# Gate logits ahead of the token mixers, as two-by-two blocks with seven products for eight

## Chip, core and metric

The kernel runs on one core of one Trainium2 chip. The metric is the device time of one execution, in microseconds; 2918.35 us is the median of three runs before the change (2917.76 to 2919.18).

## The reference

One decoder layer in float32, 512 tokens, model width 2048. The part that the change touches is the hybrid mixer: one input projection of 12560 columns, whose last 3 x 2048 columns are the logits of three gates, and the merge of three branches by these gates.

```python
proj = xn @ w_in                                  # xn: 512 x 2048
dn_qkv, dn_z, dn_a, dn_b, swa_q, swa_kv, sb_qkv, gates = split_cols(proj, IN_SIZES)
...                                               # y_dn (1024), y_swa (512), y_sb (512)
gate = jax.nn.sigmoid(gates).reshape(bsz, seq, N_BRANCH, D_MODEL)
merged = gate[:, :, 0] * (y_dn @ w_br_dn) + gate[:, :, 1] * (y_swa @ w_br_swa) + gate[:, :, 2] * (y_sb @ w_br_sb)
return merged @ w_o
```

After it come the cross attention into 256 memory tokens, a convolutional FFN and the final norm, which the change leaves alone.

## The kernel before

Activations lie feature-major: a tile holds 128 features by 512 tokens, and the normalized input xn is 16 such tiles, each kept as a sum of two tiles of the fast 32-bit matmul type, `hi` and `lo` (called xh and xl in the code). A dense product of 128 output features is `dense`: for each of 16 k-tiles of the weights, three matmuls of 512 columns add wh x hi, wh x lo and wl x hi into one PSUM bank. The weights come as 512 KB `raw` tiles on SP's queue (three buffers); for four k-tiles at a time ScalarE (ACT) casts wh, and VectorE (DVE) forms wl = raw - wh (four buffers each). These loads, casts and subtractions have high priority, so the scheduler that orders each engine's instructions puts them well ahead of their use; it fixes one order per engine, and an engine takes its instructions in that order.

The stages are: transposes of mem and x with the memory projections on PE (until about 84 us), the gated DeltaNet, sliding window and stick-breaking attention (four heads, to about 853 us), the merge (region `p_c`, to about 1557 us), output projection, cross attention, FFN. In the merge, for each of 16 output tiles m and each branch b, the gate's dense product of 48 matmuls runs, ACT takes its sigmoid into `sg`, then the branch's dense product of 8, 4 or 4 k-tiles runs, DVE multiplies the two, and POOL adds the branches. The branch inputs y (16 tiles, y15 from the last stick-breaking head) are split into yh and yl at m = 0. The gate products depend on xn alone, so the scheduler places the first of them between the steps of the last stick-breaking head. In that head `z` are the scores (L651), `ops` the output (L686).

PSUM has eight banks: `acc` (two) for dense products, `gps` (six in the attention stage) for all else.

Of the kernel before, what the change touches and what calls it, by code (L numbers as in the profile page):

```python
# [17 lines left out]
P = 128  # L18
# [40 lines left out]
def decoder_kernel(ctx: ExitStack, tc: tile.TileContext, x, mem, norm_mix, w_in, dn_conv, dn_a_log, dn_dt_bias, dn_norm,  # L59
# [11 lines left out]
    main = ctx.enter_context(tc.tile_pool(name="main", bufs=1))  # L71
    rawp = ctx.enter_context(tc.tile_pool(name="rawp", bufs=3))
    wsp = ctx.enter_context(tc.tile_pool(name="wsp", bufs=4))
    misc = ctx.enter_context(tc.tile_pool(name="misc", bufs=2))
    psd = ctx.enter_context(tc.tile_pool(name="psd", bufs=2, space=bass.MemoryType.PSUM))
    psum = ctx.enter_context(ExitStack())
    gen = []

    def gen_pool(name, bufs):
# [5 lines left out]
    def dense_ps():  # L85
        return psd.tile([P, S], F32, name="acc")
# [11 lines left out]

# [1 line left out]
    def constant(where, name, col, w=P, queue=nc.gpsimd):  # L100
# [18 lines left out]
    hi = [None] * KT  # L119
    lo = [None] * KT  # L120

    def split_slot(k):
        hi[k] = main.tile([P, S], F32R, name=f"hi{k}")
        lo[k] = main.tile([P, S], F32R, name=f"lo{k}")
        return hi[k], lo[k]

    def mrg_tile(k):
        return main.tile([P, S], F32, name=f"mrg{k}")

# [42 lines left out]

# [121 lines left out]
    gen_pool("psg_dn", 3)  # L294
    y = [None] * 16
    with region("p_dn") as dp:
# [90 lines left out]
        for h0 in range(0, DNH, 2):  # L387
# [25 lines left out]
            act.activation(dt, dt, AF.Exp)  # L413
            # keys
            kd, junk = wide("kd"), dp.tile([P, P], BF16, name="junk", bufs=1)
# [39 lines left out]
            for lvl in range(LEVELS):  # L455
# [94 lines left out]

# [1 line left out]
    with tc.issue_after(last.ins):  # L552
# [137 lines left out]

# [1 line left out]
    mrg = [None] * KT  # L692
    with region("p_c") as cp:
        yh, yl = [None] * 16, [None] * 16
        for m in range(KT):
            for b, (w, k0, nk) in enumerate(((w_br_dn, 0, 8), (w_br_swa, 8, 4), (w_br_sb, 12, 4))):
                acc = dense_ps()
                dense(acc, w_in, 0, KT, O_G + b * D + m * P, xh, xl)
                sg = misc.tile([P, S], F32, name="sg")
                last = act.activation(sg, acc, AF.Sigmoid)  # L700
                if m == 0:
                    for k in range(k0, k0 + nk):
                        yh[k] = cp.tile([P, S], F32R, name=f"yh{k}", bufs=1)
                        yl[k] = cp.tile([P, S], F32R, name=f"yl{k}", bufs=1)
                        split(yh[k], yl[k], y[k])
                acc = gen_ps()
                dense(acc, w, 0, nk, m * P, yh[k0:k0 + nk], yl[k0:k0 + nk])
                if b == 0:
                    mrg[m] = mrg_tile(m)
                    dve.tensor_tensor(mrg[m], acc, sg, op=ALU.mult)  # L710
                else:
                    t = misc.tile([P, S], F32, name="m0")
                    dve.tensor_tensor(t, acc, sg, op=ALU.mult)  # L713
# [4 lines left out]
    def token_rstd(sq, o, t):  # L718
# [24 lines left out]
    with region("p_e") as ep:  # L743
# [25 lines left out]
        for h in range(4):  # L769
# [37 lines left out]
            ol.append(l_)  # L807
# [1 line left out]
    NCH = 4  # L809
    with region("p_g") as gp:  # L810
# [20 lines left out]
        def up_pair(j):  # L831
            res = []
            for s, c in enumerate((j, 32 + j)):
                acc = dense_ps()
                dense(acc, w_up, 0, KT, c * P, hh, hl)
                v = gp.tile([P, S], F32, name="v")
                dve.tensor_tensor(v, acc, rstd, op=ALU.mult)  # L837
                u = gp.tile([P, S], F32, name="u", bufs=3)
                act.activation(u, v, AF.Copy, scale=ffcw[:, 128 + c:129 + c])  # L839
                for i in (1, 0):  # L840
                    sh = 2 - i
                    w = ffcw[:, 64 * i + c:64 * i + c + 1]
# [6 lines left out]
            where, tags = (main, (f"mrg{2 * n}", f"mrg{2 * n + 1}")) if n < 8 else (gp, (f"ah{n}", f"al{n}"))  # L849
# [97 lines left out]
```

## Time and profile before

| | |
|---|---|
| median of three runs | 2918.35 us (2917.76 to 2919.18) |
| the profiled execution | span 2917.2 us; as the runs go some 1.2 us more in its own time |
| granted TensorE clock, mean | 0.996 |
| busy share PE / DVE / ACT / POOL | 98% / 45% / 36% / 9% |
| merge stage, 853 to 1558 us | 3105 matmuls of 512 columns |
| HBM | 266.41 MB read, 4.19 MB written, 93 GB/s over the span |

In the lines of the profile, L153 is line 153 of the kernel above. A row of the groups gives line, engine, operation, output tile and input tiles, shapes, how often, then the busy time in us, the mean duration in ns, and the idle time ahead with the engine that ended it. A row of the timeline begins with the start and the duration in us; a row with xN joins N neighbours. Matmuls overlap: one of 512 columns lasts 0.39 us, but the next may start before it ends, and the distance from start to start is what counts.

### The profile page before, as it was taken

How to read it: one execution, taken by the hardware profiler on the slowest of the kernel's cores; microseconds unless marked ns; L12 is line 12 of the kernel's file. 1: busy time of each engine (PE TensorE's matmuls, PEld its weight loads, DVE VectorE, ACT ScalarE, POOL GpSimd, SP SyncE). 2: the span in 40 equal slices, each digit the busy share in tenths (PEclk: the TensorE clock that was granted, in tenths of full speed). 3: DMA queues.
4: the chain of work that ended last, by engine and by line, in shares of the span. 5: the costliest groups of instructions: out<-in, count | busy, mean ns of one | idle time of the engine just before them, and what ended most of it. 6: DMA issues, size and time to landing. Idle time of an engine off the chain costs nothing.

```text
span 2917.2 us, 34620 instructions
## 1 busy us (share of the span) xinstructions
PE 2867.7 (98%) x13463; PEld 2365.3 (81%) x13463; DVE 1322.4 (45%) x2305; ACT 1046.6 (36%) x1926; POOL 260.0 (9%) x195
## 2 busy tenths in 40 slices
PE   7999999999999999999999999999999999999998
PEld 7787887877778888888888887788888888888887
DVE  7466576336334223223224344544344434443445
ACT  6444344334443222222224334533223323322333
POOL 2100010100000000000000110201001000000002
PEclk9999999999999999999999999999999999999999
DMA  6322212232223333333334432333333333333333
GB/s 206 103 65 73 56 53 73 64 86 65 73 76 98 94 98 98 94 98 98 94 98 124 118 97 73 91 97 99 95 101 94 99 97 94 101 94 96 99 94 116
DMA packets 469941, 272.84 MB, mean 94 GB/s; under 512 B 11249, under 2 KB 450018, under 8 KB 469138
## 3 DMA queue, kind: packets, MB, share of 16 engines
q1 hardware_dynamic: 468576, 268.60, 32.4%
q8 instruction: 105, 1.72, 0.2%
q0 software_dynamic: 560, 1.79, 0.2%
q14 instruction: 58, 0.48, 0.0%
q10 hardware_dynamic: 642, 0.26, 0.0%
HBM read 266.41 MB, written 4.19 MB: 93 GB/s over the span
## 4 chain that ended last, share of the span: by engine, by line
PE 88%; DVE 3%; ACT 1%; issue 1%; POOL 1%; ACTq 0%; DVEq 0%; POOLq 0%
PE acc L155 21%; PE acc L153 21%; PE acc L154 21%; PE gps L875 4%; PE gps L873 4%; PE gps L874 4%; PE gps L153 2%; PE gps L155 2%; PE gps L154 2%; PE gps L471 1%; PE gps L466 1%; DVE wl L150 1%; PE gps L593 0%; PE gps L686 0%; PE gps L651 0%
## 5 line engine op out<-in xcount | busy, mean ns | idle before, releaser
L153 PE MATMUL acc<-hi,wh 128*128 128x512 f32 x2912 | 1140.8, 392 | 0.7 <-ACT hi L132 0.7
L154 PE MATMUL acc<-lo,wh 128*128 128x512 f32 x2912 | 1141.2, 392 | 0.0
L155 PE MATMUL acc<-hi,wl 128*128 128x512 f32 x2912 | 1141.2, 392 | 0.0
L150 DVE TENSOR_TENSOR wl<-raw,wh 128x512 fp32r<-128x512 f32 x826 | 589.0, 714 | 940.5 <-ACT wh L149 917.9
L149 ACT CAST wh<-raw 128x512 fp32r<-128x512 f32 x840 | 521.7, 622 | 1304.7 <-PE acc L154 1093.0
L155 PEld LDWEIGHTS acc<-hi,wl 128*128 128x128 f32 x2912 | 547.9, 188 | 113.0 <-issue 2.3
L153 PEld LDWEIGHTS acc<-hi,wh 128*128 128x128 f32 x2912 | 547.6, 188 | 113.3 <-issue 1.6
L154 PEld LDWEIGHTS acc<-lo,wh 128*128 128x128 f32 x2912 | 547.8, 188 | 111.6 <-issue 0.9
L868 DVE TENSOR_TENSOR wl<-raw,wh 128x512 fp32r<-128x512 f32 x112 | 77.7, 694 | 165.2 <-ACT wh L867 145.0
L867 ACT CAST wh<-raw 128x512 fp32r<-128x512 f32 x112 | 69.8, 623 | 206.7 <-PE gps L874 171.9
L875 PE MATMUL gps<-wl,mrg 128*128 128x512 f32 x368 | 143.3, 389 | 0.0
L873 PE MATMUL gps<-wh,mrg 128*128 128x512 f32 x368 | 143.2, 389 | 0.0
L874 PE MATMUL gps<-wh,mrg 128*128 128x512 f32 x368 | 143.2, 389 | 0.0
L847 POOL TENSOR_TENSOR u<-u 128x512 f32<-128x512 f32 x32 | 58.3, 1823 | 900.8 <-ACT wh L149 801.2
L714 POOL TENSOR_TENSOR mrg<-mrg,m 128x512 f32<-128x512 f32 x32 | 52.2, 1632 | 641.9 <-DVE m L713 641.9
L843 DVE SCALAR_TENSOR_TENSOR u<-v,ffcw,u 128x511 f32<-128x511 f32 (+1 forms) x128 | 96.1, 751 | 14.6 <-ACT u L839 12.3
L153 PE MATMUL gps<-yh,wh 128*128 128x512 f32 x256 | 99.8, 390 | 0.0
L155 PE MATMUL gps<-yh,wl 128*128 128x512 f32 x256 | 99.7, 389 | 0.0
L154 PE MATMUL gps<-yl,wh 128*128 128x512 f32 x256 | 99.7, 389 | 0.0
L837 DVE TENSOR_TENSOR v<-acc,rstd 128x512 f32<-128x512 f32 x64 | 44.3, 692 | 100.5 <-PE acc L155 100.5
L875 PEld LDWEIGHTS gps<-wl,mrg 128*128 128x128 f32 x368 | 69.1, 188 | 14.4
L874 PEld LDWEIGHTS gps<-wh,mrg 128*128 128x128 f32 x368 | 69.1, 188 | 14.3
(425 smaller groups left out, 2537.0 us busy)
## 6 DMA issues: line engine op xcount, KB each, us to landing
raw<-in_w_in_dram SPq DMA_DIRECT2D x196, 512.0 KB, 3.8
raw<-in_w_up_dram SPq DMA_DIRECT2D x128, 512.0 KB, 4.0
raw<-in_w_down_dram SPq DMA_DIRECT2D x64, 512.0 KB, 3.8
raw<-in_w_o_dram SPq DMA_DIRECT2D x32, 512.0 KB, 4.1
raw<-in_w_xkv_dram SPq DMA_DIRECT2D x16, 512.0 KB, 5.0
raw<-in_w_br_dn_dram SPq DMA_DIRECT2D x16, 512.0 KB, 4.0
xraw<-in_x_dram SPq DMA_DIRECT2D x4, 1024.0 KB, 9.3
raw<-in_w_br_swa_dram SPq DMA_DIRECT2D x16, 256.0 KB, 2.7
```

The lines of the kernel that those rows point to most:

```text
L149: act.copy(wh, raw[:, s0:s0 + 4, :])
L150: (pool if share and s0 else dve).tensor_tensor(wl, raw[:, s0:s0 + 4, :], wh.bitcast(F32), op=ALU.subtract)
L153: pe.matmul(acc, wh[:, j, :], hs[k], start=(k == 0), stop=False)
L154: pe.matmul(acc, wh[:, j, :], ls[k], start=False, stop=False)
L155: pe.matmul(acc, wl[:, j, :], hs[k], start=False, stop=(k == nk - 1))
L843: dve.scalar_tensor_tensor(u[:, sh:S], v[:, 0:S - sh], w, u[:, sh:S], op0=ALU.mult, op1=ALU.add)
L847: pool.tensor_tensor(res[0], res[0], res[1], op=ALU.mult)
L867: act.copy(wh, raw[:, i, :])
L868: dve.tensor_tensor(wl, raw[:, i, :], wh.bitcast(F32), op=ALU.subtract)
L873: pe.matmul(acc, ah[j][:, ts], wh, start=(k == 0), stop=False)
L874: pe.matmul(acc, al[j][:, ts], wh, start=False, stop=False)
L875: pe.matmul(acc, ah[j][:, ts], wl, start=False, stop=(k == 7))
```

## The change

A new stage `p_gate` stands between the memory projections and the DeltaNet. It computes all gate logits and sigmoids and stores them to DRAM; the merge loads each 256 KB gate tile back as `sg` instead of computing it. The 16 k-tiles fall into two halves, an output pair is 256 columns of weights (two tiles of 128), and the 512 tokens fall into two halves of 256. So a pair is a two-by-two block product, done with seven block products of eight k-tiles (Winograd's form of Strassen's scheme). Each block product has per k-tile one matmul of 512 columns, wh with the moving block's hi and lo parts side by side, and one of 256 columns, wl with hi. The hi and lo results lie in two halves of a bank, which `fold` adds.

Four of the moving blocks are differences of quarters of xn. They are formed once, into fb0 to fb7, on DVE and ACT at the stage's start. Three of the weight blocks are the raw weights' (sraw, 1 MB each, three buffers), the others sums and differences that DVE forms per pair (`combine`, tiles sm). swh and swl, the split of 8 k-tiles at once (1024 columns), have two buffers each. The pair's banks sa, sb, sc, sd have two buffers each: all of PSUM. So the pools of the dense products (mrgp, rawp, wsp, psd) are closed before the stage and opened again behind it, and the stage's tiles use their memory. `misc` tile s7 is named sg, as the merge's loaded gates are. hi and lo of one k-tile are now halves of one tile x.

```diff
     def split_slot(k):
-        hi[k] = main.tile([P, S], F32R, name=f"hi{k}")
-        lo[k] = main.tile([P, S], F32R, name=f"lo{k}")
+        both = main.tile([P, 2, S], F32R, name=f"x{k}")
+        hi[k], lo[k] = both[:, 0, :], both[:, 1, :]
+        xb[k] = both
...
+    psum.close()
+    std.close()
+    HT = S // 2
+    gate_d = [[None] * KT for _ in range(3)]
+    with region("p_gate") as gp, tc.tile_pool(name="psw", bufs=2, space=bass.MemoryType.PSUM, reuse_waits="tile") as pw:
+        fb = [gp.tile([P, 2, 4, HT], F32R, name=f"fb{k}", bufs=1) for k in range(8)]
+        banks = {n: [pw.tile([P, S], F32, name=n) for _ in range(2)] for n in ("sb", "sd")}
+        for n in ("sb", "sd"):
+            for t in banks[n]:
+                pe.matmul(t, xh[0][:, 0:P], xh[0], start=True, stop=True)
+        for k in range(8):
+            u = gp.tile([P, 2, S], F32, name="g")
+            for j in range(2):
+                dve.tensor_tensor(u[:, j, :], xh[k + 8 * j].bitcast(F32), xl[k + 8 * j].bitcast(F32), op=ALU.add)
+            b11, b12, b21, b22 = (u[:, j, t * HT:(t + 1) * HT] for j in range(2) for t in range(2))
+            v = gp.tile([P, 4, HT], F32, name="sm")
+            for i, (p_, q_) in enumerate(((b12, b11), (b22, v[:, 0, :]), (b22, b12), (b21, v[:, 1, :]))):
+                dve.tensor_tensor(v[:, i, :], p_, q_, op=ALU.subtract)
+            act.copy(fb[k][:, 0, :, :], v)
+            dve.tensor_tensor(fb[k][:, 1, :, :], v, fb[k][:, 0, :, :].bitcast(F32), op=ALU.subtract)
...
+        def product(acc, w, of, first):
+            wh = gp.tile([P, 8, P], F32R, name="swh")
+            wl = gp.tile([P, 8, P], F32R, name="swl")
+            with tc.high_priority(1000000):
+                act.copy(wh, w)
+                dve.tensor_tensor(wl, w, wh.bitcast(F32), op=ALU.subtract)
+            av = acc.rearrange("p (h c) -> p h c", h=2)
+            for k in range(8):
+                m = of(k)
+                pe.matmul(av, wh[:, k, :], m, start=(first and k == 0), stop=False, skip_group_check=True)
+                pe.matmul(av[:, 0, :], wl[:, k, :], m[:, 0, :], start=False, stop=(k == 7), skip_group_check=True)
...
+            a, b, c, d = (pw.tile([P, S], F32, name=n) for n in ("sa", "sb", "sc", "sd"))
+            product(a, a11, B11, True)
+            act.copy(b, a)
+            product(c, combine(a11, a21, ALU.subtract), T3, True)
+            s1 = combine(a21, a22, ALU.add)
+            s2 = combine(s1, a11, ALU.subtract)
+            s7 = misc.tile([P, S], F32, name="sg")
+            act.copy(s7, c)
+            product(b, s2, T2, False)
+            product(a, a12, B21, False)
+            act.copy(d, b)
+            la = gp.tile([P, HT], F32, name="la")
+            act.copy(la, a[:, HT:S])
+            fold(out[:, 0, 0:HT], a[:, 0:HT], la)
+            product(d, s1, T1, False)
+            t = misc.tile([P, S], F32, name="m0")
+            dve.tensor_tensor(t, d, s7, op=ALU.add)
+            fold(out[:, 1, HT:S], t[:, 0:HT], t[:, HT:S])
+            product(b, a22, T4, False)
...
+            product(d, combine(a12, s2, ALU.subtract), B22, False)
...
+        for m in range(0, KT, 2):
+            for b_ in range(3):
+                g = gp.tile([P, 2, S], F32, name="g")
+                strassen_pair(w_in, O_G + b_ * D + m * P, g)
+                act.activation(g, g, AF.Sigmoid)
+                gd = dram.tile([P, 2, S], F32, name=f"gate{b_}_{m}")
+                pool.dma_start(out=gd, in_=g)
+                gate_d[b_][m], gate_d[b_][m + 1] = gd[:, 0, :], gd[:, 1, :]
...
-                acc = dense_ps()
-                dense(acc, w_in, 0, KT, O_G + b * D + m * P, xh, xl)
                 sg = misc.tile([P, S], F32, name="sg")
-                last = act.activation(sg, acc, AF.Sigmoid)
+                nc.sync.dma_start(out=sg, in_=gate_d[b][m])
```

How the order of the instructions changes is shown at three places. The first is DVE behind the memory projections. Before, the last weight splits of these (L150) led over to the DeltaNet's first ones:

```order
L275 COPY rsb<-gps 128x256
L150 TENSOR_TENSOR wl<-raw,wh 128x512 x2
L310 TENSOR_TENSOR wh<-raw,wh 128x8x16 x2
L150 TENSOR_TENSOR wl<-raw,wh 128x512 x4
L326 TENSOR_TENSOR abt<-gps,abt 128x64
```

Now the combined blocks stand there, some 50 rows for eight k-tiles, of which these are the first of the second and third (fb_1036 is fb0, x_518 and x_582 the xn tiles 2 and 10):

```order
L317 TENSOR_TENSOR fb_1036<-sm,fb_1036 128x1024
L315 TENSOR_TENSOR sm<-g,sm 128x256
L311 TENSOR_TENSOR g<-x_518 128x512
L334 TENSOR_TENSOR swl<-sraw,swh 128x1024
L315 TENSOR_TENSOR sm<-g,sm 128x256
L311 TENSOR_TENSOR g<-x_582 128x512
L315 TENSOR_TENSOR sm<-g 128x256 x2
L317 TENSOR_TENSOR fb_1037<-sm,fb_1037 128x1024
```

Between fb0's row and the swl of the second product stand 12 operations of L311, 26 of L315, 7 of L317, the swl of the first product and one combine.

The second place is a gate's work on DVE. Before, in the merge, a tile's three multiplications with the weight splits between them:

```order
L710 TENSOR_TENSOR mrg_7763<-gps,sg 128x512
L150 TENSOR_TENSOR wl<-raw,wh 128x512 x5
L713 TENSOR_TENSOR m_7855<-gps,sg 128x512
L150 TENSOR_TENSOR wl<-raw,wh 128x512 x5
L713 TENSOR_TENSOR m_7948<-gps,sg 128x512
```

Now one pair of the new stage, from the swl of its second product (first row) to that of its seventh (last row):

```order
L334 TENSOR_TENSOR swl<-sm,swh 128x1024
L342 TENSOR_TENSOR g<-sd,la 128x256
L357 TENSOR_TENSOR sm<-sm,sraw 128x1024
L334 TENSOR_TENSOR swl<-sm,swh 128x1024
L334 TENSOR_TENSOR swl<-sraw,swh 128x1024
L334 TENSOR_TENSOR swl<-sm,swh 128x1024
L357 TENSOR_TENSOR sm<-sraw,sm 128x1024
L357 TENSOR_TENSOR sm<-sraw 128x1024
L334 TENSOR_TENSOR swl<-sraw,swh 128x1024
L342 TENSOR_TENSOR g<-sa,la 128x256
L376 TENSOR_TENSOR m_1958<-sd,sg 128x512
L334 TENSOR_TENSOR swl<-sm,swh 128x1024
```

The combine in the third row is s2, which stands behind swl of the second product and a fold of the pair before; c7 and the next pair's c2 (L357, seventh and eighth row) stand ahead of swl of the sixth product. The same stretch on ACT, from the next pair's first and second cast on; the sigmoid of the pair before stands ahead of the third product's cast:

```order
L333 CAST swh<-sraw 128x1024
L333 CAST swh<-sm 128x1024
L384 COPY la<-sd 128x256
L391 ACTIVATE g<-g 128x1024
L362 COPY sb<-sa 128x512
L333 CAST swh<-sm 128x1024
L333 CAST swh<-sraw 128x1024
L367 COPY sg<-sc 128x512
```

L362 is the copy b<-a of the new pair; the third product's cast (sixth row) stands behind it and the sigmoid.

The third place is PE in the last stick-breaking head. Before, matmuls of the first gate filled the steps of the head (the rows on hi and lo are the gate's):

```order
L640 MATMUL gps<-ident,svt 128x128 x4
L153 MATMUL acc<-hi_497,wh 128x512
L154 MATMUL acc<-lo_498,wh 128x512
L155 MATMUL acc<-hi_497,wl 128x512
L651 MATMUL gps<-sq,sk 128x512
L651 MATMUL gps<-sq,sk 128x384
L651 MATMUL gps<-sq,sk 128x256
L153 MATMUL acc<-hi_506,wh 128x512
```

Now the head's rows follow one another (L764 scores, L783 to L792 the sums, L799 the output), and the first branch product comes behind the last; the rows between are left out here after the first of them:

```order
L753 MATMUL gps<-ident,svt 128x128 x4
L764 MATMUL gps<-sq,sk 128x512
L764 MATMUL gps<-sq,sk 128x384
L764 MATMUL gps<-sq,sk 128x256
L764 MATMUL gps<-sq,sk 128x128
L783 MATMUL gps<-sph,tri_lr 128x512
```

```order
L799 MATMUL gps<-sz,svv 128x512
L799 MATMUL gps<-sz,svv 128x384
L799 MATMUL gps<-sz,svv 128x256
L799 MATMUL gps<-sz,svv 128x128
L165 MATMUL acc<-yh_11340,wh 128x512
```

Nothing of the dense work is left that depends on xn alone, so the places between are empty.

More of the change, by code (lines that the diff above doesn't have):

```diff
@@ L71, in decoder_kernel, with open_std @@
     main = ctx.enter_context(tc.tile_pool(name="main", bufs=1))
-    rawp = ctx.enter_context(tc.tile_pool(name="rawp", bufs=3))
-    wsp = ctx.enter_context(tc.tile_pool(name="wsp", bufs=4))
     misc = ctx.enter_context(tc.tile_pool(name="misc", bufs=2))
-    psd = ctx.enter_context(tc.tile_pool(name="psd", bufs=2, space=bass.MemoryType.PSUM))
+    dram = ctx.enter_context(tc.tile_pool(name="dram", bufs=1, space=bass.MemoryType.DRAM))
+    std = ctx.enter_context(ExitStack())
     psum = ctx.enter_context(ExitStack())
     gen = []
+    mrgp = rawp = wsp = psd = None
+    def open_std(n):
+        nonlocal mrgp, rawp, wsp, psd
+        psum.close()
+        std.close()
+        mrgp, rawp, wsp = (std.enter_context(tc.tile_pool(name=f"{name}{n}", bufs=bufs, reuse_waits="tile"))
+                           for name, bufs in (("mrgp", 1), ("rawp", 3), ("wsp", 4)))
+        psd = std.enter_context(tc.tile_pool(name=f"psd{n}", bufs=2, space=bass.MemoryType.PSUM, reuse_waits="tile"))
+    open_std(0)
     def gen_pool(name, bufs):
@@ L120, in decoder_kernel @@
     lo = [None] * KT
+    xb = [None] * KT
     def split_slot(k):
-        hi[k] = main.tile([P, S], F32R, name=f"hi{k}")
-        lo[k] = main.tile([P, S], F32R, name=f"lo{k}")
+        both = main.tile([P, 2, S], F32R, name=f"x{k}")
+        hi[k], lo[k] = both[:, 0, :], both[:, 1, :]
+        xb[k] = both
         return hi[k], lo[k]
     def mrg_tile(k):
-        return main.tile([P, S], F32, name=f"mrg{k}")
+        return mrgp.tile([P, S], F32, name=f"mrg{k}")
     def split(h, l, src, gain=None):
@@ L174, in decoder_kernel @@
     with region("p_start") as ps:
-        memT = [main.tile([P, S], F32R, name=f"mrg{k}") for k in range(KT)]
+        memT = [mrgp.tile([P, S], F32R, name=f"mrg{k}") for k in range(KT)]
         memraw = [ps.tile([P, D], F32, name="memraw", bufs=2) for _ in range(2)]
@@ L282, in decoder_kernel, with moving, of, fold @@
         pool.dma_start(out=dst, in_=src[0].partition_broadcast(P))
+    psum.close()
+    std.close()
+    HT = S // 2
[16 more added lines that the diff above has]
+            dve.tensor_tensor(fb[k][:, 1, :, :], v, fb[k][:, 0, :, :].bitcast(F32), op=ALU.subtract)
+        def moving(form):
+            def of(k):
+                if form < 3:
+                    j, t = ((0, 0), (1, 0), (1, 1))[form]
+                    return xb[k + 8 * j][:, :, t * HT:(t + 1) * HT]
+                return fb[k][:, :, form - 3, :]
+            return of
+        B11, B21, B22, T1, T2, T3, T4 = (moving(i) for i in range(7))
+        def product(acc, w, of, first):
[9 more added lines that the diff above has]
+                pe.matmul(av[:, 0, :], wl[:, k, :], m[:, 0, :], start=False, stop=(k == 7), skip_group_check=True)
+        def fold(dst, half, other):
+            dve.tensor_tensor(dst, half, other, op=ALU.add)
+        def strassen_pair(w, col, out):
+            raw = []
+            with tc.high_priority(1000000):
+                for h in range(2):
+                    r = gp.tile([P, 8, 2 * P], F32, name="sraw", bufs=3)
+                    nc.sync.dma_start(out=r, in_=w[h * 8 * P:(h + 1) * 8 * P, col:col + 2 * P].rearrange("(k p) c -> p k c", p=P))
+                    raw.append(r)
+            a11, a21 = raw[0][:, :, 0:P], raw[0][:, :, P:2 * P]
+            a12, a22 = raw[1][:, :, 0:P], raw[1][:, :, P:2 * P]
+            def combine(x_, y_, op):
+                s_ = gp.tile([P, 8, P], F32, name="sm")
+                with tc.high_priority(1000000):
+                    dve.tensor_tensor(s_, x_, y_, op=op)
+                return s_
+            a, b, c, d = (pw.tile([P, S], F32, name=n) for n in ("sa", "sb", "sc", "sd"))
[17 more added lines that the diff above has]
+            product(b, a22, T4, False)
+            t = misc.tile([P, S], F32, name="m0")
+            dve.tensor_tensor(t, b, s7, op=ALU.add)
+            fold(out[:, 1, 0:HT], t[:, 0:HT], t[:, HT:S])
+            product(d, combine(a12, s2, ALU.subtract), B22, False)
+            la = gp.tile([P, HT], F32, name="la")
+            act.copy(la, d[:, HT:S])
+            fold(out[:, 0, HT:S], d[:, 0:HT], la)
+        for m in range(0, KT, 2):
[6 more added lines that the diff above has]
+                gate_d[b_][m], gate_d[b_][m + 1] = gd[:, 0, :], gd[:, 1, :]
@@ L285, in conv_silu @@
+    open_std(1)
     def conv_silu(dst, acc, c):
@@ L705, in decoder_kernel @@
                         split(yh[k], yl[k], y[k])
-                acc = gen_ps()
+                acc = dense_ps()
                 dense(acc, w, 0, nk, m * P, yh[k0:k0 + nk], yl[k0:k0 + nk])
@@ L731, in add_square @@
             pool.tensor_tensor(sq, sq, t, op=ALU.add)
-    with tc.issue_after(last.ins):
-        act.preload_act_table_set("natural_log_exp_and_others")
     tail = ctx.enter_context(region("p_tail"))
@@ L848, in up_pair @@
             n = j % 10
-            where, tags = (main, (f"mrg{2 * n}", f"mrg{2 * n + 1}")) if n < 8 else (gp, (f"ah{n}", f"al{n}"))
+            where, tags = (mrgp, (f"mrg{2 * n}", f"mrg{2 * n + 1}")) if n < 8 else (gp, (f"ah{n}", f"al{n}"))
             ah[j] = where.tile([P, S], F32R, name=tags[0], bufs=1)
```

## The prediction

> **What bounds the kernel now.** I read the page's engine shares first, then the chain that ended last, then the groups by line, then the windows, and last the timeline around the three places that the change touches.
>
> ```profile
> span 2917.2 us, 34620 instructions
> PE 2867.7 (98%) x13463; PEld 2365.3 (81%) x13463; DVE 1322.4 (45%) x2305; ACT 1046.6 (36%) x1926; POOL 260.0 (9%) x195
> PE 88%; DVE 3%; ACT 1%; issue 1%; POOL 1%; ACTq 0%; DVEq 0%; POOLq 0%
> L153 PE MATMUL acc<-hi,wh 128*128 128x512 f32 x2912 | 1140.8, 392 | 0.7 <-ACT hi L132 0.7
> ```
> ```profile
> 853.00:1558.00 705.00, 704.16 (x3105) 581.39 (x3104) 231.23 (x346) 213.63 (x351) 53.77 (x35) 1.00 0.35 96
> ```
>
> PE is busy 98% of the span and 88% of the chain; the dense matmuls scarcely wait. The second fence is the merge stage (columns: length, then busy time and instructions of PE, PEld, DVE, ACT, POOL, then granted clock, DMA share, GB/s). PE never stops there, so one matmul of 512 columns costs 705.00/3105 = 0.227 us, and every one taken away is worth that much. DVE has two thirds of that stage free. So the change trades PE's time, which is the bound, for DVE and ACT work, which was cover; the question is whether it stays cover.
>
> **A. The gates leave the merge stage.** 48 gates of 48 matmuls, 2304 x 0.227 = **-523 us**. Their casts, wl subtractions and sigmoids lie beside PE and are worth nothing themselves. What stays there is 768 branch matmuls (174 us): per four k-tiles 12 x 0.227 = 2.72 us of PE against one cast and one subtraction,
>
> ```profile
> L149 ACT CAST wh<-raw 128x512 fp32r<-128x512 f32 x840 | 521.7, 622 | 1304.7 <-PE acc L154 1093.0 <-PE gps L154 111.2 <-issue 60.0
> L150 DVE TENSOR_TENSOR wl<-raw,wh 128x512 fp32r<-128x512 f32 x826 | 589.0, 714 | 940.5 <-ACT wh L149 917.9 <-PE gps L874 6.1 <-PE gps L640 6.1
> L713 DVE TENSOR_TENSOR m<-gps,sg 128x512 f32<-128x512 f32 x32 | 22.1, 691 | 50.9 <-PE gps L155 50.9
> ```
>
> so those stay hidden: 0.62 on ACT, 0.71 (at most 1.4 with the product) on DVE.
>
> **B. The 24 tile pairs.** One product is 8 k-tiles, each a matmul of 512 and one of 256 columns. The short one's pitch is in the memory projections:
>
> ```profile
> 52.19 0.28 PE L153 MATMUL acc<-mrg,wh 128*128 128x256 f32 x1
> 53.51 0.28 PE L155 MATMUL acc<-mrg,wl 128*128 128x256 f32 x1
> ```
>
> Eleven steps in 1.32 us, 0.120 each. A product is 8 x 0.347 = 2.78 us and a pair 7 x 2.78 = 19.45 us on PE; 24 pairs at that pace are 467 us. (Before, a pair was 96 x 0.227 = 21.8 us: the products save 2.3 us, 11%, not one eighth, since the short matmul's pitch is more than half.) Can the other engines follow? The nearest rows, in ns:
>
> ```profile
> L439 DVE TENSOR_TENSOR am<-e,bl 128x1024 f32<-128x1024 f32 x4 | 4.9, 1218 | 0.1
> L477 DVE TENSOR_TENSOR dt<-gps,dt 128x1024 f32<-128x1024 f32 x4 | 4.9, 1225 | 1.9 <-PE gps L476 1.9
> L412 ACT ACTIVATE e<-e 128x1024 f32<-128x1024 f32 x4 | 4.2, 1062 | 0.9 <-DVE e L409 0.9
> L413 ACT ACTIVATE dt<-dt 128x1024 f32<-128x1024 f32 x4 | 4.2, 1052 | 0.0
> L468 ACT COPY am<-gps 128x512 f32<-128x512 f32 x32 | 17.2, 589 | 39.8 <-PE gps L466 39.8
> L654 ACT COPY sz<-gps 128x256 f32<-128x256 f32 x4 | 1.5, 373 | 1.0 <-DVE sz L652 1.0
> L614 DVE TENSOR_TENSOR ws<-ws,wst 128x256 f32<-128x256 f32 x4 | 1.7, 426 | 0.1
> ```
>
> DVE per pair: 7 swl and 4 combines at 1.22, 4 folds at 0.42, 2 sums at 0.69: 16.5 us. ACT: 7 casts and a sigmoid at 1.05, three copies at 0.59, two at 0.37: 10.9 us. Both are under 19.45, so neither is full; but swh and swl have two buffers, so product n+2's cast may start only when product n has ended, and then cast, subtraction and product stand in a row. The links between engines:
>
> ```profile
> 999.61 0.62 ACT L149 CAST wh<-raw 128x512 fp32r<-128x512 f32 x1 [2.10 <-PE acc L154]
> 1000.27 0.69 DVE L150 TENSOR_TENSOR wl<-raw,wh 128x512 fp32r<-128x512 f32 x1 [2.03 <-ACT wh L149]
> 1001.90 0.39 PE L154 MATMUL acc<-lo,wh 128*128 128x512 f32 x1
> 1002.33 0.62 ACT L149 CAST wh<-raw 128x512 fp32r<-128x512 f32 x1 [2.10 <-PE acc L154]
> ```
>
> ACT to DVE takes 0.04, a matmul's end to ACT 0.04 after its 0.39 duration, that is 0.20 after PE is free for the next. Now from the end of product 7 (t = 0), in the order that the engines have: swh2 on ACT 0.20-1.25, swl2 on DVE 1.29-2.51, a fold to 2.86 (0.07 overlap of neighbours), s2 to 4.01. ACT meanwhile has the sigmoid until 3.96 and b<-a until 4.45; swh3 needs s2 and stands behind both: 4.35-5.40; swl3 5.44-6.66. Products 1 and 2 end at 5.56, so product 3's second matmul waits 1.03 us. Product 3 ends at 9.37, and with it frees swh5: 9.57-10.62, swl5 to 11.88, c7 to 13.14, the next pair's c2 to 14.36, swl6 14.33-15.55. Product 6 would have started at 14.93 and waits 0.55. Product 7 ends at 21.04. So **24 x 21.04 = +505 us**. The pace below is 19.1, if the short matmul costs half of the long (0.1135) and PE never waits. Above, DVE can be held by POOL, whose queue now has one store per pair:
>
> ```profile
> 74.05 2.42 POOL L278 TENSOR_TENSOR xk<-xk,rsb 128x1024 f32<-128x1024 f32 x1
> 74.69 2.33 DVE L150 TENSOR_TENSOR wl<-raw,wh 128x512 fp32r<-128x512 f32 x1 [1.95 <-ACT wh L149]
> ```
>
> Beside POOL's work a subtraction of 0.69 took 2.33. If a store did that once a pair, on the ring, it would be 21.04 + 1.64 = 22.7. I take 21.04: the rows of 1024 elements are of the very shapes, and a store computes nothing.
>
> **C. The gate stage's start.** The memory projections end here:
>
> ```profile
> 72.33 0.41 DVE L275 COPY rsb<-gps 128x256 f32<-128x256 f32 x1
> 84.13 0.28 PE L155 MATMUL acc<-mrg,wl 128*128 128x256 f32 x1
> 84.25 0.40 PE L315 MATMUL acc<-hi,wh 128*32 128x512 f32 x1
> 86.62 0.62 ACT L223 ACTIVATE xv<-gps,mst 128x128 f32<-128x128 f32 x2 [0.53 <-PE gps L221]
> ```
>
> Before, PE went on at once at 84.25. Now product 1 (2.8 us) is all that it has until the combined forms fb exist. They lie in memory that memT, raw and wsp hold until 84.3, and the first cast stands behind the xv activations, which end at 87.2: it ends at about 87. DVE can do the first two tiles' sums before, from 72.7 on. Between it and product 2's swl stand, in the order of DVE: 12 sums at 0.62, 26 differences at 0.35, 7 fb subtractions, swl1, one combine and swl2 at 1.15 (rows above, less 0.07): 28.0 us, to 115. PE loses 115 - 84.3 - 2.8 = 28, the four dummy matmuls 0.9, and on waking some 3:
>
> ```profile
> 56.71 2.82 PE L267 MATMUL gps<-ident,xraw 128*128 128x128 f32 x12 [2.92 <-ACT xraw L263]
> 59.54 0.42 PE L154 MATMUL acc<-mrg,wh 128*128 128x256 f32 x1
> 62.70 0.28 PE L155 MATMUL acc<-mrg,wl 128*128 128x256 f32 x1
> ```
>
> After 2.92 us of idleness the short matmul takes 0.42 until about 62.4, and 0.28 again after: about six microseconds at half speed, so about 3 lost. **+32 us** (28 if the clock stays, 36 if more of the sums wait for 84.3).
>
> The Trainium skill, TensorE: Matmul & The Clock Gate, section HAM oscillation, states that idle gaps of more than about 3.4 us halve the clock; here 2.92 did. The same section tells of a kernel whose PE paused briefly between groups while it cycled through PSUM banks, and whose clock oscillated for it. That speaks against the pairs, which do the same; it is a rival below, priced by rows alone.
>
> **D. Entry to DeltaNet.** The a/b weights' loads stand on SP behind gate loads that wait for the last pair's t, so they are issued late:
>
> ```profile
> raw<-in_w_in_dram SPq DMA_DIRECT2D x2, 64.0 KB, 2.4
> xs<-in_x_dram SPq DMA_DIRECT2D x16, 256.0 KB, 2.9
> ```
>
> 2.4 us, a cast and a subtraction: **+3.5** (0 if the load goes ahead, 5 if the queue is slower). Stores on POOL's queue and sraw loads (1 MB, two a pair, against 21 us) are costed at nothing; the third sraw buffer hides them; uncovered, a 1 MB load would be a 5 to 9 us wait per pair.
>
> **E. The last stick-breaking head.** The gate matmuls (0,0) used to run between its steps. Now nothing does.
>
> ```profile
> 771.00 2.20 PE L651 MATMUL gps<-sq,sk 128*128 128x512 f32 x6
> 789.22 2.42 PE L686 MATMUL gps<-sz,svv 128*128 128x512 f32 x8
> 874.32 2.42 PE L686 MATMUL gps<-sz,svv 128*128 128x512 f32 x8
> 876.79 0.59 ACT L688 COPY mrg<-gps 128x512 f32<-128x512 f32 x1 [2.01 <-PE gps L686]
> 877.79 4.27 ACT L132 CAST yh<-mrg 128x512 fp32r<-128x512 f32 x8
> ```
>
> In the third head scores to last product are 789.22 + 2.42 - 771.00 = 20.6 us, of which the head's own matmuls are some 6.5. That leaves 14 idle; the copy of y15 and the first yh cast, on ACT one behind the other, add 1.6; DVE-bound splits of y (16 at 0.62 with four wl) 1.5; half clock on the head's matmuls and the first dense ones 3. **+20** (14 to 24).
>
> **Sum.** -523 + 505 + 32 + 3.5 + 20 = +37.5 on the profiled execution's span of 2917.2; its own time is 1.2 more, as the median 2918.35 is. 2954.7 + 1.2 = **2956 us**. Break-even is a pair of (523 - 55.5)/24 = 19.48 us, PE's own pace: without a single wait in the pairs the change would just pay for its entry and exit.
>
> **Rivals.**
> R1, the other side: PE never waits in the pairs. For it: DVE and ACT have room (16.5 and 10.9 of 19.45), and each of the two rings is late by little. Against: the order of the queues as built, and the size of what must vanish: taking the sigmoid's 1.05 away would shorten only product 3's ring until swl2, the fold and s2 set it (4.01 against 4.35), 0.3 of the 1.0. The rows of 1024 would have to be 0.7 instead of 1.22. At 19.45 the sum is -1 (2918); with the short matmul at 0.1135, 19.1 a pair, it is -9, 2909. From 19.24 down it is faster by more than 0.2%.
> R2: the stores hold DVE. At 22.7 a pair it is 24 x 1.64 = +39 more, 2995; off the ring half of the time, 2976. The Trainium skill, SBUF — State Buffer, section SBUF: two separate sides, says that GpSimd and a DVE operation with two SBUF inputs lock each other out of a shared port pair; the row above agrees, but whether a store's descriptors count no run here shows yet.
> R3: the gates arrive late in the merge. sg has two buffers; that of (m, 2) is issued once (m, 0) has been multiplied, and is needed 5.7 us later; issue and 2.9 us of landing leave some 1.4. If loads behind others take 3 us longer, 1.6 x 16 tiles = +26, 2982.
> R4: the two stalls per pair (1.0 and 0.6 us) bring the clock down. At 3 us lost after each second stall as above, 24 x 3 = +72, 3028. Against: the stall in the fence took 2.92 us, three times these.
>
> **How the numbers follow.** Forecast 0.66, R1 0.11, R2 0.13, R3 0.07, R4 0.03. The likeliest case's own range is 2940 to 2972 (pair 20.5 to 21.6, C and E at their ends). A run's own spread here is 0.05%, and about 0.2% (5.8 us) is what a comparison can tell from no change. Faster: R1 with the short matmul at half the long, 0.07; same: the rest of R1 and the tail of the forecast towards it, 0.07; slower 0.86. The range leaves out most of R1, R4 and R2's end: 2918 to 2988.
>
> **What would show it.** In the gate stage: a pair every 21.0 us, product 3 starting about 1.0 late and product 6 0.55 late, both waiting for DVE's swl; DVE busy 0.78 of the stage; some 28 us without PE after 84 us and half clock behind it; a gap of 14 us before the first branch matmul of the merge; elsewhere nothing changed. Wrong would be a pair at 19.5 (R1), a swl of 1.22 drawn out to 2 or more beside a store (R2), PE in the merge waiting for sg (R3), a granted clock under 0.95 within the pairs (R4).

## The result, and the profile after

The changed kernel takes 2948.93 us (median of four runs, 2946.58 to 2949.97) against 2918.76 of the kernel before in the same comparison: a ratio of 1.0104, 95% interval 1.0089 to 1.0118. It is 30 us slower; the forecast was 2956, slower by 37.5.

The page of the changed kernel, engine shares and granted clock:

```profile
span 2946.7 us, 35935 instructions
PE 2838.1 (96%) x13851; PEld 2347.4 (80%) x13851; DVE 1593.6 (54%) x2577; ACT 1154.8 (39%) x2002; POOL 270.3 (9%) x219
PEclk9799999999999999999999999999999999999999
```

PE does less work than before (2838 us busy for 2868), but its share has fallen from 98 to 96%: it now stands idle for longer than it saved. The stretches of the gate stage and of the merge (length, busy time and instructions of PE, PEld, DVE, ACT, POOL, granted clock, DMA share, GB/s):

```profile
84.30:115.39 31.09, 7.11 (x24) 5.04 (x23) 27.12 (x50) 10.74 (x14) 0.00 (x0) 0.61 0.00 0
300.00:400.00 100.00, 96.05 (x541) 82.35 (x540) 73.83 (x82) 49.48 (x63) 2.66 (x5) 1.00 0.43 132
1385.00:1425.00 40.00, 27.01 (x93) 18.67 (x92) 21.92 (x34) 20.87 (x33) 3.22 (x5) 0.79 0.16 47
1425.00:1590.00 165.00, 165.00 (x730) 136.58 (x729) 78.61 (x122) 45.56 (x77) 49.27 (x31) 1.00 0.58 171
```

The first row is the start of the gate stage: PE works 7 of 31 us while DVE works 27. The second is the stage in steady state: 4 us in a hundred without PE, at a full clock. The third holds the last stick-breaking head: 13 of 40 us without PE, at a granted clock of 0.79. The fourth is the merge, where PE never stops.

Four marks divide both spans: the end of the memory projections (84.25 before, 84.30 after), the first matmul on the a/b weights (84.25; 619.53), the last head's first score matmul (853.27; 1387.16), the first matmul of the output projection (1557.23; 1587.17).

| stretch | before | after | difference | forecast |
|---|---|---|---|---|
| gate stage, exit included | 0 | 535.2 | +535.2 | B + C + D = +540.5 |
| a/b weights to the last head's scores | 769.0 | 767.6 | -1.4 | 0 |
| scores to output projection | 704.0 | 200.0 | -504.0 | A + E = -503 |
| from there to the end | 1360.0 | 1359.5 | -0.4 | 0 |
| sum | | | +29.5 | +37.5 |

The rows that the marks are from, with the steady pairs (a pair's second product is the only one that writes sc, so its first matmul marks the pair):

```profile
115.39 0.80 PE L338 MATMUL sc<-fb,swh 128*128 128x512 f32 x1 [20.20 <-ACT swh L333]
307.78 0.39 PE L338 MATMUL sc<-fb,swh 128*128 128x512 f32 x1
328.58 0.39 PE L338 MATMUL sc<-fb,swh 128*128 128x512 f32 x1
613.78 0.39 PE L338 MATMUL sd<-x,swh 128*128 128x512 f32 x1
619.53 0.40 PE L428 MATMUL acc<-x,wh 128*32 128x512 f32 x1 [2.81 <-DVE wh L423]
1387.16 2.20 PE L764 MATMUL gps<-sq,sk 128*128 128x512 f32 x6 [0.53 <-ACT sq L750]
1587.17 0.39 PE L165 MATMUL acc<-x,wh 128*128 128x512 f32 x1
```

A pair takes 328.58 - 307.78 = 20.80 us, and did so over the last sixteen. 24 of them are 499.2. The last product starts at 613.78 and ends 2.78 later, at 616.56; to 619.53 there are 3.0. What is left of 535.2 is 33.0, the start with the first pairs: the second product starts 115.39 - 84.30 - 2.77 = 28.3 late, and the first pairs take 4.7 longer than the steady ones. With A as worked out, E is 523 - 504 = 19.0; the expectations below say 18.5 for it, since they count from the head's second score matmul (1387.69) instead of its first.

### The profile page after: what moved, and what is told of

Same layout as the page of the kernel before. It is cut to its first block, busy times and chain, and to the rows that moved or that the text cites. A ratio compares the mean times of both kernels' runs of the same rounds, so it can differ in the third digit from the quotient of the medians.

```text
span 2946.7 us, 35935 instructions
## 1 busy us (share of the span) xinstructions
PE 2838.1 (96%) x13851; PEld 2347.4 (80%) x13851; DVE 1593.6 (54%) x2577; ACT 1154.8 (39%) x2002; POOL 270.3 (9%) x219
## 4 chain that ended last, share of the span: by engine, by line
PE 69%; DVE 4%; ACT 2%; issue 1%; POOL 0%; ACTq 0%; DVEq 0%; POOLq 0%
PE acc L167 16%; PE acc L166 16%; PE acc L165 16%; PE gps L984 4%; PE gps L983 4%; PE gps L982 4%; PE gps L584 1%; PE gps L579 1%; DVE wl L162 1%; PE gps L706 0%; PE gps L799 0%; ACT junk L641 0%; DVE st L175 0%; PE gps L764 0%; PE gps L735 0%
## 5 line engine op out<-in xcount | busy, mean ns | idle before, releaser
L165 PE MATMUL acc<-x,wh 128*128 128x512 f32 x2144 | 840.3, 392 | 0.7 <-ACT x L144 0.7
L166 PE MATMUL acc<-x,wh 128*128 128x512 f32 x2144 | 840.5, 392 | 0.0
L167 PE MATMUL acc<-x,wl 128*128 128x512 f32 x2144 | 840.3, 392 | 0.0
L161 ACT CAST wh<-raw 128x512 fp32r<-128x512 f32 x648 | 402.1, 622 | 911.4 <-PE acc L166 799.1
L162 DVE TENSOR_TENSOR wl<-raw,wh 128x512 fp32r<-128x512 f32 x634 | 454.4, 718 | 544.3 <-ACT wh L161 523.6
L165 PEld LDWEIGHTS acc<-x,wh 128*128 128x128 f32 x2144 | 402.7, 188 | 83.1 <-issue 1.3
L167 PEld LDWEIGHTS acc<-x,wl 128*128 128x128 f32 x2144 | 402.8, 188 | 82.9 <-issue 2.1
L166 PEld LDWEIGHTS acc<-x,wh 128*128 128x128 f32 x2144 | 402.9, 188 | 82.0 <-issue 0.9
L334 DVE TENSOR_TENSOR swl<-sm,swh 128x1024 fp32r<-128x1024 f32 x96 | 117.4, 1223 | 119.6 <-ACT swh L333 119.6
L977 DVE TENSOR_TENSOR wl<-raw,wh 128x512 fp32r<-128x512 f32 x112 | 78.5, 701 | 166.0 <-ACT wh L976 145.7
L976 ACT CAST wh<-raw 128x512 fp32r<-128x512 f32 x112 | 69.8, 624 | 207.5 <-PE gps L983 172.8
L338 PE MATMUL sa<-x,swh 128*128 128x512 f32 x384 | 138.1, 398 | 2.2 <-ACT swh L333 2.2
L338 PE MATMUL sb<-fb,swh 128*128 128x512 f32 x384 | 138.6, 395 | 1.6 <-ACT sb L362 1.6
L339 PE MATMUL sb<-fb,swl 128*128 128x256 f32 x384 | 112.3, 292 | 17.5 <-DVE swl L334 17.3
```

What stands on the lines that cost most here:

```text
L161: act.copy(wh, raw[:, s0:s0 + 4, :])
L162: (pool if share and s0 else dve).tensor_tensor(wl, raw[:, s0:s0 + 4, :], wh.bitcast(F32), op=ALU.subtract)
L165: pe.matmul(acc, wh[:, j, :], hs[k], start=(k == 0), stop=False)
L166: pe.matmul(acc, wh[:, j, :], ls[k], start=False, stop=False)
L167: pe.matmul(acc, wl[:, j, :], hs[k], start=False, stop=(k == nk - 1))
L334: dve.tensor_tensor(wl, w, wh.bitcast(F32), op=ALU.subtract)
```

## The experiments

Four of the runs each take away one loss of the ledger, or the seven-product scheme itself. Two more test a cause, one changes the order inside a product, and two put the findings together.

**Three buffers of swh and swl.**

```diff
-            wh = gp.tile([P, 8, P], F32R, name="swh")
-            wl = gp.tile([P, 8, P], F32R, name="swl")
+            wh = gp.tile([P, 8, P], F32R, name="swh", bufs=3)
+            wl = gp.tile([P, 8, P], F32R, name="swl", bufs=3)
...                              # tiles g and la: bufs=1
```

> The changed kernel with three buffers instead of two for swh and swl (g and la have one instead of two, to make room). If the 1.4 us that PE waits per pair come from the rings of two buffers (cast, subtraction and product in a row), a pair falls from 20.80 to PE's own 19.45 to 19.6, and the time from 2949 by 24 x 1.3 = 31 to about 2918, as before the change. Rival: the order of the combines on DVE (s2 behind a fold, c7 and c2 ahead of the sixth swl) sets the starts whatever the buffers; then a pair stays over 20.5 and the time over 2940. Rival: the one g tile brings a new wait on the store; then PE waits for a fold, and a pair is over 21.

Measured 2930.72 us (1.0046 of before, 1.0031 to 1.0061): 18 less than the changed kernel, not 31. The waits of PE between 300 and 400 us (waiting line, what it waited for, us in all, times, longest), first of the changed kernel:

```profile
PE sb L339 <- DVE swl L334: 4.0, 9, 0.7
```

With three buffers the same view has no line, and the window has PE at 100%:

```profile
300.00:400.00 100.00, 100.00 (x568) 86.78 (x568) 78.66 (x87) 52.56 (x67) 2.65 (x5) 1.00 0.40 132
301.72 0.40 PE L338 MATMUL sc<-fb,swh 128*128 128x512 f32 x1
321.51 0.40 PE L338 MATMUL sc<-fb,swh 128*128 128x512 f32 x1
119.47 0.79 PE L338 MATMUL sc<-fb,swh 128*128 128x512 f32 x1 [21.19 <-ACT swh L333]
```

So the rings of two buffers are what PE waited for, and the order of the combines is not. But a pair without waits is 321.51 - 301.72 = 19.79 us, not 19.45: a product takes 2.83. That leaves -24 in the pairs. The start is 4 us longer (119.47 for 115.39), since with one g tile the next block's sums wait for the last; and PE waits 6.4 at the exit, for 2.8. There ACT's first instruction behind the stage waits for the last gate's store to land, as its row shows:

```profile
601.28 0.30 ACT L475 CAST ones_r<-ones 128x128 fp32r<-128x128 f32 x1 [3.43 <-DMA gate<-g]
```

**All eight products, in the same place.** The gate stage with no combined blocks: per pair four times eight k-tiles of three matmuls of 512 columns.

```diff
-        fb = [gp.tile([P, 2, 4, HT], F32R, name=f"fb{k}", bufs=1) for k in range(8)]
...
+            acc = [pw.tile([P, S], F32, name=n) for n in ("sa", "sc")]
+            for h in range(2):
+                for j in range(2):
...                              # swh, swl from raw[h][:, :, j * P:(j + 1) * P]
+                    for k in range(8):
+                        q = 8 * h + k
+                        pe.matmul(acc[j], wh[:, k, :], xh[q], start=(q == 0), stop=False)
+                        pe.matmul(acc[j], wh[:, k, :], xl[q], start=False, stop=False)
+                        pe.matmul(acc[j], wl[:, k, :], xh[q], start=False, stop=(q == KT - 1))
```

> The gates computed ahead as in the changed kernel, but with all eight products: per pair 96 matmuls of 512 columns from weights split in tiles of 1024, no combined blocks, no combines, no folds. By the ledger: a pair 96 x 0.227 = 21.8 instead of 20.80, +24 us; the 28 us without PE and the 4.7 of the first pairs go but for some 4; the exit to DeltaNet (4.6) and the uncovered head (18.5) stay. 2949 + 24 - 29 = 2944. Rival: moving the gates is free and the products alone cost; then it is back at 2918 to 2922. Rival: the seven products are worth a full eighth (2.7 a pair); then 2949 + 41 - 29... = 2985 less the head, at least 2960.

Measured 2947.81 (1.0104, 1.0089 to 1.0119), where 2944 was expected. In the stage PE never waits; what it loses lies at the exit (5.8, where ACT waits 4.5 for the last gate's store, as with three buffers), in the head, and 4.5 at the entry:

```profile
90.00:600.00 510.00, 510.00 (x2245) 422.16 (x2244) 114.07 (x94) 122.03 (x140) 12.25 (x23) 1.00 0.38 118
PE acc L374 <- DVE wh L369: 5.8, 1, 5.8
PE sa L321 <- ACT swh L317: 4.5, 1, 4.5
PE gps L729 <- ACT sph L144: 7.0, 1, 7.0
```

This is the move without the scheme, and it costs 30 us. The scheme itself, as it was built, is worth nothing: its 24 us in the pairs went into its own start.

**Two pairs left in the merge**, so that their matmuls can run inside the last head.

```diff
+                if (m, b_) not in ((0, 0), (0, 1)):
...
+                if gate_d[b][m] is None:
+                    acc = dense_ps()
+                    dense(acc, w_in, 0, KT, O_G + b * D + m * P, xh, xl)
+                    act.activation(sg, acc, AF.Sigmoid)
+                else:
+                    nc.sync.dma_start(out=sg, in_=gate_d[b][m])
...
-                acc = dense_ps()
+                acc = gen_ps()
```

> The changed kernel, but the gates of output tiles 0 and 1 of the first two branches stay in the merge as dense products of 48 matmuls, so that two of them can run between the steps of the last stick-breaking head (branch products accumulate in the gps banks, as before the change). Two pairs of 20.8 become 21.8 each, +2; the last head's 18.5 come back: 2949 - 16.5 = 2932. Rival: what holds the merge's start is the chain of y15's copy and the splits of y on ACT and DVE, which no matmul shortens; then half comes back, 2940.

Measured 2931.38 (1.0047, 1.0032 to 1.0062), 17.5 less than the changed kernel, where 16.5 less was expected. The waits of PE from 1300 to 1640 us, of the changed kernel first (from 1380; four more of 0.4 to 0.7 make 13.0 in all), then of this one:

```profile
PE gps L783 <- ACT sph L144: 7.0, 1, 7.0
PE gps L799 <- ACT sz L796: 2.0, 1, 2.0
PE acc L165 <- ACT yh L144: 1.2, 1, 1.2
PE acc L166 <- DVE yl L145: 0.8, 2, 0.6
```
```profile
PE gps L819 <- ACT scuh L144: 1.7, 2, 0.8
```

The waits for sph, for the exponentials (sz) and for yh and yl are gone. The chain of y15's copy and the splits is hidden too, since the second gate's matmuls run on behind the head; so this run does not tell the idle places of the head from that chain. By the waits of the changed kernel the chain is the smaller part: 2.4 (yh, yl and the first product on DVE) of the 13.0. What the branch products' other banks do to the time was not measured apart.

**Two plain pairs at the start**, emitted ahead of the combined blocks.

```diff
+        plain = [plain_pair(w_in, O_G + b_ * D + m * P) for m, b_ in [(0, 0), (0, 1)]]
         for k in range(8):
             u = gp.tile([P, 2, S], F32, name="g")
```

> The changed kernel with the first two pairs computed plainly (96 matmuls of 512 columns, on xn alone), emitted ahead of the combined blocks, so that PE has 43.6 us of work while DVE forms them. Of the 33 us at the start some 5 stay (until the first cast and subtraction have come), and the two pairs cost 1.0 more each: 2949 - 28 + 2 = 2923. Rival: DVE, which has eight more subtractions among the blocks (9 us), falls behind and PE waits for it in the plain products or the first combined ones; then no more than 15 come back, 2934 or more.

Measured 2924.45 (1.0024, 1.0014 to 1.0033), 24.5 less. PE's waits from 80 to 200 us are all that is left of the start:

```profile
PE sa L326 <- ACT swh L322: 1.7, 1, 1.7
PE sb L376 <- DVE swl L371: 1.3, 2, 0.7
PE gps L233 <- ACT m L230: 0.5, 1, 0.5
PE sa L328 <- DVE swl L323: 0.2, 1, 0.2
```

The 20.2 of the changed kernel in front of sc is no longer among them: DVE had time for the blocks.

**The sigmoid out of the pairs**, applied to the loaded gate tile in the merge.

```diff
-                act.activation(g, g, AF.Sigmoid)
...
                 nc.sync.dma_start(out=sg, in_=gate_d[b][m])
+                act.activation(sg, sg, AF.Sigmoid)
```

> The changed kernel with the sigmoid taken out of the pairs and applied to the loaded gate tile in the merge. ACT then has b<-a and the third product's cast free at once. By the ring worked out in the prediction the third product's wait shrinks by 0.3 us only, because s2 on DVE ends at 4.0 and the cast waits for it: a pair 20.5 instead of 20.80, 2949 - 7 = 2942. Rival: ACT's queue sets the third product's start; then its wait of 0.94 goes whole, 2949 - 22 = 2927. In the merge the sigmoid (0.6 of each 3.6 us on ACT) is hidden; if not, it adds up to 16 x 0.6.

Measured 2940.40 (1.0078, 1.0061 to 1.0094): 8.5 less, where 7 was expected, and the rival's 22 is out. PE's waits from 300 to 400 us:

```profile
PE sb L339 <- DVE swl L334: 1.9, 6, 0.4
```

They fell from 4.0 to 1.9 us. The third product's cast now starts when s2 comes from DVE, as the prediction's ring has it:

```profile
303.89 1.05 ACT L333 CAST swh<-sm 128x1024 fp32r<-128x1024 f32 x1 [0.40 <-DVE sm L357]
```

Of the products without a wait, 40 take 2.77 here and 53 take 2.83 (200 to 585 us), so a part of what the waits gave went into the pace (pairs of 20.5 to 20.7).

**The gate tiles loaded on POOL's queue**, to take them out of the way of the a/b weights.

```diff
-                nc.sync.dma_start(out=sg, in_=gate_d[b][m])
+                nc.gpsimd.dma_start(out=sg, in_=gate_d[b][m])
```

> The changed kernel with the gate tiles loaded in the merge through POOL's queue instead of SP's. The a/b weights are then loaded ahead, and the 2.8 us without PE at the entry to DeltaNet and the half clock behind it (1.6) go: 2944.5. But on POOL a load stands behind the additions of the merge (1.6 us each): if the slack of a gate tile is the 1.4 us that the prediction worked out for SP's queue, PE waits at each third gate, up to 16 x 1.6 = 26 us, 2960 to 2970. If no wait shows in the merge, the slack was larger than that.

Measured 2950.15 (1.0111, 1.0096 to 1.0126): no gain. The entry to DeltaNet, on SP, ACT and PE:

```profile
612.66 0.99 SPq L420 DMA_DIRECT2D raw<-in_w_in_dram  x2
617.30 1.06 ACT L391 ACTIVATE g<-g 128x1024 f32<-128x1024 f32 x1 [0.49 <-DVE g L342]
618.26 0.28 ACT L475 CAST ones_r<-ones 128x128 fp32r<-128x128 f32 x1
618.45 0.49 ACT L422 CAST wh<-raw 128x128 fp32r<-128x128 f32 x2
619.21 0.60 PE L428 MATMUL acc<-x,wh 128*32 128x512 f32 x1 [2.81 <-DVE wh L423]
```

The load was issued 2.5 us earlier than in the changed kernel (612.66 for 615.17), and PE waits 2.81 all the same: the cast of the weights stands on ACT behind the last pair's sigmoid, which waits for the last fold. In the changed kernel the two loads land 3.0 to 3.2 us after their issue, at about 618.2 and 618.8, just as ACT comes free for them (618.8). So the queue of the loads is not what holds PE; taking it away alone gives nothing. In the merge no new wait showed, though a gate now stands behind POOL's additions: the slack of a gate tile is larger than the 1.4 us worked out for it.

**The three edits together**: three buffers, two plain pairs at the start, two pairs left in the merge.

> The three edits together: three buffers of swh and swl, two pairs computed plainly at the stage's start, two pairs left in the merge for the last head. If the three losses are separate, they add: the pairs go from 20.80 to the 19.79 measured with three buffers (20 pairs, -20), the start -24.5 and the head -17.5 as measured with each alone, and the gate loads no longer stand ahead of the a/b weights, about -4: 2949 - 66 = 2883, or 1.2% faster than before the change. Rival: the losses overlap (with one g tile the blocks took 4 us longer, and what is gained at the start waits in the first pairs); then 2895 to 2905. Rival: the pace of a product is 2.78 rather than 2.83 in this one: 2876.

Measured 2887.62 (0.9899 of before, 0.9884 to 0.9914), 1.0% faster than the kernel before. The losses are separate and nearly add: 2883 was expected. The pairs stay at 19.79, and the wait at the exit is still there (2.86), which the 2883 had left out.

**The short matmuls last.** The changed kernel, with a product's loop made two.

```diff
             for k in range(8):
-                m = of(k)
-                pe.matmul(av, wh[:, k, :], m, start=(first and k == 0), stop=False, skip_group_check=True)
-                pe.matmul(av[:, 0, :], wl[:, k, :], m[:, 0, :], start=False, stop=(k == 7), skip_group_check=True)
+                pe.matmul(av, wh[:, k, :], of(k), start=(first and k == 0), stop=False, skip_group_check=True)
+            for k in range(8):
+                pe.matmul(av[:, 0, :], wl[:, k, :], of(k)[:, 0, :], start=False, stop=(k == 7), skip_group_check=True)
```

> The changed kernel with one loop made two: a product runs its eight matmuls of 512 columns (wh) first and its eight of 256 (wl) after them; buffers, engines' work and pools stay. swl is then needed 1.8 us later, and swh is free 0.96 us earlier. By the ring of waits the third product's 0.94 and the sixth's 0.45 both go with two buffers: a pair 7 x 8 x 0.347 = 19.4 if the pitches are those of the memory projections, 2949 - 24 x 1.4 = 2915, within 0.2% of the time before the change. If the slow pace of 2.83 per product, which three buffers showed (19.79 a pair), belongs to any run of products without waits, it is 2925. If the pace comes from taking long and short matmuls in turn, it goes: 2915. Rival: short matmuls in a row are bound by their weight loads (0.19 each): a product 8 x (0.227 + 0.19) = 3.3, a pair over 23, 3000.

Measured 2917.21 (0.9993, 0.9984 to 1.0002): the same as before the change, 32 us less than the changed kernel, from the order of two loops. The timeline of PE, one product:

```profile
313.05 2.00 PE L337 MATMUL sc<-fb,swh 128*128 128x512 f32 x8
314.89 1.11 PE L339 MATMUL sc<-fb,swl 128*128 128x256 f32 x8
315.85 2.00 PE L337 MATMUL sb<-fb,swh 128*128 128x512 f32 x8
```

Eight long ones take 1.84 and eight short ones 0.96 (0.120 each, so the weight loads of 0.19 do not bind them), 2.79 a product and 19.55 a pair, with no wait of PE from 150 us to the stage's end. swl has 1.8 us more until it is needed, and that is more than both rings were late by. swh is free 0.96 us earlier as well; the run changes both at once and does not tell them apart.

**All that helped, with two buffers**: short matmuls last, two plain pairs first, two pairs in the merge.

> The short matmuls last, two plain pairs at the start and two pairs left in the merge, with two buffers of swh and swl as in the change. Against the three edits together (2888) the pairs take 19.4 instead of 19.79 if the pace is that of the pitches, 20 x 0.37 = 7 us: 2880; with the slow pace as well 2888.

Measured 2882.73 (0.9880 of before, 0.9867 to 0.9894). This is the fastest of all: 1.2% under the kernel before, and 66 us under the change as it came. Its PE is at 98% of the span again, as before the change:

```profile
span 2880.5 us, 35690 instructions
PE 2824.7 (98%) x13787; PEld 2345.4 (81%) x13787; DVE 1552.2 (54%) x2533; ACT 1145.2 (40%) x1989; POOL 270.5 (9%) x217
```

## Why the prediction was right, term by term

**A and E** were to give -503 and gave -504.0: with A as worked out, E is 19.0 for 20. The sum of E was right, its parts less so, and that they came out within 1 us is in part luck. The head takes 20.8 us from the first score matmul to the end of the last product, for 20.6. But PE idles 12.5 in it and behind it (13.0 with the 0.5 ahead of the first score matmul), not 14 + 1.6 + 1.5 = 17.1. Nor is that one gap before the first branch matmul: the longest wait, 7.0, stands in the head's middle, and that matmul waits 1.2. The other 6.5, for which the prediction had 3, is left for matmuls at a lower clock (0.79 over the 40 us around the head) and for resuming after the waits. That what E lost was cover is shown by the two pairs left in the merge, which bring all of it back; how much of it is the chain of copies behind the head, that run leaves open.

**B**, 21.04 a pair, was 20.80; -5.8 over 24 pairs is most of the 8 us by which the forecast was high. The two waits came where the ring had them, both for swl:

```profile
310.55 0.39 PE L338 MATMUL sb<-fb,swh 128*128 128x512 f32 x1
311.60 0.39 PE L339 MATMUL sb<-fb,swl 128*128 128x256 f32 x1 [0.66 <-DVE swl L334]
L334 DVE TENSOR_TENSOR swl<-sm,swh 128x1024 fp32r<-128x1024 f32 x96 | 117.4, 1223 | 119.6 <-ACT swh L333 119.6
L333 ACT CAST swh<-sm 128x1024 fp32r<-128x1024 f32 x96 | 100.6, 1048 | 134.9 <-PE sb L338 51.8 <-PE sd L338 41.3 <-issue 34.9
```

The third product starts at 310.55, and its second matmul at 311.60 where 310.78 would have been next: 0.8, and 0.94 with the resuming (its start to the next product's is 3.71, not 2.77). The sixth lost 0.45. Forecast were 1.03 and 0.55. The durations taken from the rows of 1024 elements held to the hundredth: 1.22 on DVE, 1.05 on ACT.

**C**, 32, was 33.0. DVE's 28 us of work up to the second product's swl took 29.5, from 87.05 to 116.6 in the trace (seven L317 are in it with fb0's own, at 87.05; between fb0's row and that swl stand six); product 2 started at 115.39, and the clock stood at half until about 122. The plain pairs show that it is the missing cover and not the sums' price that counts: behind 43.6 us of PE work the same sums no longer hold PE.

**D**, 3.5, was 3.0, right in size and wrong in cause. The step that failed is "the a/b weights' loads stand on SP behind gate loads ..., so they are issued late": late they are, but that alone is not what PE waits for. The run with the loads on POOL's queue had them 2.5 us earlier and the same 2.81 of waiting: what ends last is the cast on ACT, behind the sigmoid and the fold of the last product.

**The rivals.** R1, PE without a wait, is not how the kernel as changed runs, but the two experiments that made it so measured its price: 2917 with the short matmuls last, as R1's 2918 had it; with three buffers 2931, because start and exit grew and the pace was 19.79. R2, stores that hold DVE: swl took 1211 to 1227 ns in all 168 cases. That alone is no test, because in the changed kernel each store of the 23 pairs before the last is issued while DVE stands idle. The run with the sigmoid out of the pairs is one: there each of these stores is issued in the midst of s2, which reads two tiles of SBUF, and s2 took 1215 or 1216 ns.

```profile
302.58 1.22 DVE L357 TENSOR_TENSOR sm<-sm,sraw 128x1024 f32<-128x1024 f32 x1
302.96 0.54 POOL L392 DMA_DIRECT2D gate<-g  x1 [19.98 <-DVE g L342]
```

So a store's issue does not hold DVE in this case. The rule of the Trainium skill, SBUF — State Buffer, section SBUF: two separate sides, about the shared port is for a GpSimd operation that reads SBUF, where DVE's has two SBUF inputs; these rows agree with that if a store's issue is no such operation.

R3, late gates: no PE wait in the merge beyond one of 0.4. R4, a clock that falls for the short stalls: 1.00 from 200 to 600 us. So two stalls in 20.8 us, of 0.94 and 0.45, do not halve it. The Trainium skill, TensorE: Matmul & The Clock Gate, section A second HAM failure mode: psum-queue depth-cycling (behind the section that the prediction names), tells of brief pauses between groups for which a kernel's clock oscillated; this trace shows none of that. The pause of 2.81 at the exit did halve it:

```profile
619.53 0.40 PE L428 MATMUL acc<-x,wh 128*32 128x512 f32 x1 [2.81 <-DVE wh L423]
620.95 0.63 PE L428 MATMUL acc<-x,wh 128*32 128x512 f32 x1
623.88 0.39 PE L427 MATMUL acc<-x,wh 128*16 128x512 f32 x1
```

Behind it the a/b matmuls lasted 0.63 until about 623.5, and 0.39 after (granted clock 0.50 from 620.4 to 623.8). But the length of a pause alone does not decide. With two pairs left in the merge the same wait of 2.81 stands at the same place, and the clock stays at 1.00 (577.4 to 583):

```profile
577.41 0.40 PE L459 MATMUL acc<-x,wh 128*32 128x512 f32 x1 [2.81 <-DVE wh L454]
579.96 0.40 PE L459 MATMUL acc<-x,wh 128*32 128x512 f32 x1
```

In the kernel before, a pause of 2.32 us (up to 286.72) was followed by half clock from 287.9 to 291.3, and one of 3.30 (up to 494.30) by none. So the 3.4 us that the Trainium skill, TensorE: Matmul & The Clock Gate, section HAM oscillation, gives for an idle gap is not a safe bound in this case: shorter pauses can halve the clock and need not. What else decides was not found.

What the prediction did not weigh is the order inside a product. It counted swl as needed by the second matmul, which is how the loop has it, and took the two buffers for the ring's cause. Both more buffers and the other order take the waits away; the order does it without more memory.

## What to carry to other kernels

Fewer products on the bound engine are worth what is left once their entry, their exit and the work that they used to cover have been paid: here 24 us of 523, against 33, 3 and 19. A dense stage that depends on nothing is cover; before it is moved ahead in one piece, find what it ran beside, and leave a part of it there. And where a stage waits for the second of two operands, let the matmuls that need only the first go first.

## What had not been expected of the hardware

The pace of a product has more than one value with the same instructions. In the changed kernel products take 2.77 or 2.83 us, and the pace changed only across a wait: from 131 to 260 us both occur, and every one of the back-to-back products after 262 took 2.77. With three buffers, where PE does not wait, all from 183 us on took 2.83 (0.353 a k-tile), with no other clock shown (1.00) and no wait. Long and short matmuls in separate runs took 2.79. With three buffers the next matmul starts 0.237 behind a long one, in the changed kernel at its faster pace 0.230; behind a short one it is 0.117 in both. What sets the pace was not separated. A changed kernel's pair without its two stalls is 20.80 - 0.94 - 0.45 = 19.41, so over 24 pairs the slow pace is worth 24 x (19.79 - 19.41) = 9 us.
